# Two encoder layers in float32: when the heads' sums, the probabilities' parts, memory's sums and the weights' roundings are issued

## Chip, core and metric

The kernel runs on one core of a Trainium2 chip. The metric is the device time of one execution in microseconds; the median of several runs counts. The engines are TensorE (PE; its weight loads are PEld), VectorE (DVE), ScalarE (ACT), GpSimd (POOL) and SyncE (SP, which issues the DMAs here).

## What is computed

Two layers over 512 positions of 1024 values, and a final normalisation. Cut to what matters:

```python
for l in range(2):
    x = x + hybrid_mixer(rms_norm(x, norm_mix[l]), w_in[l], ...)      # 8 neighbourhood heads (8 x 16 window)
                                                                      # + 8 grouped-query heads, 2 key/value heads
    x = x + memory_cross_attention(rms_norm(x, norm_mem_q[l]), rms_norm(mem, norm_mem_kv[l]), ...)  # 4 heads, 256 tokens
    x = x + conv_ffn(rms_norm(x, norm_ffn[l]), ...)                   # SwiGLU, width-3 convolution, 2816 wide
return rms_norm(x, norm_final)

# the grouped-query heads: each query and key head is RMS-normalised, then rotated
g_q = apply_axial_rope(rms_norm(g_q, q_norm), cos, sin)
g_k = apply_axial_rope(rms_norm(g_k, k_norm), cos, sin)
```

## The kernel before

**Numbers in two parts.** All is float32. For a product each operand is split into a rounded high part and the low remainder, and three matmuls are made (`mm3`: high x high, high x low, low x high); attention probabilities and values use two parts stored side by side. A weight is loaded by SP into one of two `raw` tiles, rounded to `hi` by ACT (L265) and subtracted to `lo` by POOL, for a few by DVE (L266), in `emit_split`. `get_w` asks for the next weight and emits the splits of those up to two further on; `plan` fixes the order of weights. A PSUM result is split in `split_psum`: ACT rounds (L473), DVE subtracts (L474).

**Order.** TensorE's and SP's instructions keep the order in which they are written. Those of ACT, DVE and POOL are ordered by a planner that takes, among the steps it thinks ready, the one written first; `behind(n)` gives a step a place n instructions later (or earlier, when n is negative). `W_BEHIND` is 45 for most roundings of weights.

**Attention as a weave.** `weave` runs steps of the units (scores, normalise, transpose, values) with delays between them, and at each `None` a `Filler` runs pieces of other TensorE work, up to a quantum of nanoseconds (`NA_FILL`, `GQA_FILL`): input projections, grouped-query projections, the output projection of the neighbourhood heads (`out_na`), the memory keys and values, and the first rows of the closing product (`close_rows`). A piece ends at a `yield`, and each piece ticks `late`, which calls functions put off by so many pieces. `Counted` adds up the nanoseconds of matmuls that quanta are measured by; a matmul counts at least 107.

**Rotated heads.** `gqa_project` makes a group's projection in two pieces of 12 matmuls of 512 columns. `gqa_rope` scales it (L843, L844 on DVE) and squares it (L845 on ACT). Then, put off: `swap` (four DMAs that exchange rows); one piece later `rotate` (column sums of the squares on TensorE, the matmuls on `pairs`; L858 on DVE; the power -1/2, L864, and its copy, L865, on POOL; the addition L866 on POOL); two pieces later `norm` (four matmuls on `ident` that turn the copy); one piece later `split` (L876). The groups are k, 0, 1, v, 2, 3, where v has no rotation.

**PSUM.** Eight banks: four `mm`, two `sc` (scores), two `tr` (transposes, sums and small products).

**Memory.** `mem_stat`, in layer 0 alone, loads the memory tokens, squares them on ACT (L541), sums the squares of eight chunks on DVE by two reductions (L542) and an addition (L543), sums over partitions on TensorE, takes the power, and spreads the result (`mem_rep`, L556). `MEM_STEPS` says at which steps of the second attention its pieces, and those of `memory_prepare`, come.

**Closing rows.** The last product before a normalisation ends row by row. `Norm.close` adds the residual (L429), copies the row (L430), makes the next product's operand, high part on ACT (L439) and low part on DVE (L441), and squares the row (L445 on ACT, then L453 and L456, additions on POOL or DVE). `fold` adds the two parts of a head pair's output and puts off its split (L492 on ACT, L493 on POOL).

## Time and profile before

| what | value |
|---|---|
| median of 3 runs | 1382.12 us (1381.91 to 1383.89) |
| profiled execution | 1382.43 us, of which the span is 1380.3 us |
| mean granted TensorE clock | 0.994 |
| busy: PE, DVE, ACT, POOL | 1352.6, 862.9, 673.4, 701.9 us |
| chain that ended last | 91% PE |

The span runs from the first to the last instruction of the program. A row of a timeline reads: start, duration, engine, line, operation, out<-in, size, count, and in brackets the idle time of the engine before it with what ended it. A row of the waits reads: who waited, for whom, microseconds in total, how often, the longest. "L474" is line 474 of the kernel before.

### The profile page before, as it was taken

Reading aid. Unit: us, or ns where it says so; the run is one execution under the profiler, and the core shown is the slowest. Engines: PE = TensorE matmul, PEld = TensorE weight load, DVE = VectorE, ACT = ScalarE, POOL = GpSimd, SP = SyncE. Lnnn points to the kernel's source line nnn. Section 1 sums busy time; section 2 is a strip of 40 time slices with the busy share of each in tenths; the row PEclk is TensorE's granted clock in tenths of the full one; section 3 lists DMA queues with packets and bytes.
Section 4 is the critical chain, followed back from the end, with each engine's and each line's share of the span. In section 5 each row is a group of like instructions: output and inputs, shape, how many; then the busy total and the mean of one; then the engine's idle time right before and its main releaser. Section 6 shows DMA issues by size and latency. Waiting matters only on the chain.

```text
span 1380.3 us, 19215 instructions
## 1 busy us (share of the span) xinstructions
PE 1352.6 (98%) x7072; PEld 1155.5 (84%) x7072; DVE 862.9 (63%) x1522; ACT 673.4 (49%) x1255; POOL 701.9 (51%) x521
## 2 busy tenths in 40 slices
PE   9999899999999999999999999999999999999997
PEld 7898689888888888888888978897888888888897
DVE  6666766564886188268546557745748833861874
ACT  6765577464543243233546646755644423432441
POOL 2457676626444443443635577756364444444441
PEclk9999999999999999999999999999999999999999
DMA  6653312222333333332455531223133333333331
GB/s 215 203 146 85 99 47 77 92 61 77 107 93 93 106 92 88 109 94 87 121 140 171 139 106 55 72 72 102 53 96 96 92 104 95 90 94 107 91 94 62
DMA packets 218205, 138.83 MB, mean 101 GB/s; under 512 B 6016, under 2 KB 211072, under 8 KB 218112
## 3 DMA queue, kind: packets, MB, share of 16 engines
q1 hardware_dynamic: 217968, 137.60, 34.2%
q8 instruction: 56, 0.92, 0.3%
q14 instruction: 37, 0.30, 0.1%
q10 hardware_dynamic: 144, 0.00, 0.0%
HBM read 125.00 MB, written 2.10 MB: 92 GB/s over the span
## 4 chain that ended last, share of the span: by engine, by line
PE 91%; DVE 3%; ACT 2%; DMA 2%; POOL 1%; issue 1%; SPq 0%; DVEq 0%; ACTq 0%; POOLq 0%
PE mm L77 82%; PE sc L77 5%; PE tr L64 3%; PE tr L77 1%; DMA raw<-in_w_in 1%; ACT hi L265 1%; POOL lo L266 1%; DMA raw<-in_w_mem_q 1%; DVE xg L474 0%; DVE s L901 0%; DVE t L456 0%; DVE mm L429 0%; DVE t L542 0%; SPq L64 0%; DVE xT L430 0%
## 5 line engine op out<-in xcount | busy, mean ns | idle before, releaser
L266 POOL TENSOR_TENSOR lo<-raw,hi 128x1024 fp32r<-128x1024 f32 (+2 forms) x268 | 499.0, 1874 | 516.0 <-ACT hi L265 513.6
L77 PE MATMUL mm<-xg,hi 128*128 128x512 f32 x1920 | 594.3, 391 | 0.0
L77 PEld LDWEIGHTS mm<-xg,hi 128*128 128x128 f32 x1920 | 356.8, 188 | 71.9 <-ACT t L845 0.2
L265 ACT CAST hi<-raw 128x512 fp32r<-128x512 f32 (+2 forms) x276 | 224.2, 836 | 369.4 <-PE mm L77 301.9
L77 PE MATMUL mm<-xg,lo 128*128 128x512 f32 x960 | 373.8, 389 | 0.0
L77 PE MATMUL mm<-r,hi 128*128 128x512 f32 (+1 forms) x1144 | 333.1, 375 | 3.0 <-DVE xg L441 2.6
L77 PEld LDWEIGHTS mm<-r,hi 128*128 128x128 f32 x1144 | 208.3, 190 | 42.1 <-DVE xg L441 4.3
L1207 DVE SCALAR_TENSOR_TENSOR t<-t,par,t 128x7 f32<-128x7 f32 (+1 forms) x352 | 201.9, 641 | 34.0 <-ACT t L1200 34.0
L77 PE MATMUL mm<-r,lo 128*128 128x512 f32 (+1 forms) x572 | 213.7, 374 | 0.0
L77 PEld LDWEIGHTS mm<-xg,lo 128*128 128x128 f32 x960 | 180.2, 188 | 38.0
L77 PEld LDWEIGHTS mm<-r,lo 128*128 128x128 f32 x572 | 108.3, 189 | 19.1
L1192 DVE TENSOR_TENSOR t<-mm,rep 128x512 f32<-128x512 f32 x88 | 60.1, 687 | 78.0 <-PE mm L77 62.4
L480 POOL TENSOR_SCALAR t<-t,s 128x512 f32<-128x512 f32 (+1 forms) x112 | 66.2, 607 | 81.1 <-DVE s L752 42.3
L1213 DVE TENSOR_TENSOR r<-t,r 128x512 fp32r<-128x512 f32 x44 | 90.1, 2047 | 7.3 <-ACT r L1212 4.1
L1209 ACT ACTIVATE t<-t 128x512 f32<-128x512 f32 x44 | 27.9, 633 | 134.4 <-DVE t L1207 134.4
L1236 DVE TENSOR_TENSOR xT<-xT,mm 128x512 f32<-128x512 f32 x32 | 21.9, 685 | 106.8 <-PE mm L77 106.8
L77 PE MATMUL sc<-r,r 128*128 128x256 f32 (+1 forms) x352 | 72.5, 338 | 1.6 <-ACT t L903 1.6
L1200 ACT ACTIVATE t<-t,par 128x512 f32<-128x512 f32 x88 | 66.9, 806 | 3.3 <-DVE t L1192 3.3
L64 PE MATMUL tr<-ident,t 128*128 128x128 f32 x456 | 61.9, 274 | 4.8 <-DVE xg L474 1.7
L64 PEld LDWEIGHTS tr<-ident,t 128*128 128x128 f32 x456 | 52.3, 140 | 13.3 <-issue 3.5
L77 PE MATMUL mm<-r,r 128*128 128x256 f32 (+1 forms) x428 | 61.8, 297 | 0.0
L77 PEld LDWEIGHTS mm<-r,r 128*128 128x128 f32 x428 | 56.1, 191 | 2.4
(150 smaller groups left out, 1571.5 us busy)
## 6 DMA issues: line engine op xcount, KB each, us to landing
raw<-in_w_up SPq DMA_DIRECT2D x88, 512.0 KB, 3.7
raw<-in_w_in SPq DMA_DIRECT2D x33, 512.0 KB, 4.4
raw<-in_w_down SPq DMA_DIRECT2D x32, 448.0 KB, 3.6
raw<-in_w_mem_kv SPq DMA_DIRECT2D x16, 512.0 KB, 3.8
raw<-in_w_down SPq DMA_DIRECT2D x16, 512.0 KB, 4.0
r<-in_bias SPq DMA_DIRECT2D x16, 384.0 KB, 5.5
r<-r SPq DMA_DIRECT2D x22, 256.0 KB, 5.1
raw<-in_w_out SPq DMA_DIRECT2D x8, 512.0 KB, 3.6
```

What stands on the lines that cost most here:

```text
L64: return lambda *a, **k: self.tc.keep_in_program_order(op(*a, **k))
L77: return self.tc.keep_in_program_order(self.engine.matmul(out, lhsT, rhs, **k))
L265: act.copy(hi[:, k], raw[:, k])
L266: (POOL if eng[0] == "P" else DVE).tensor_sub(lo[:, k], raw[:, k], f(hi)[:, k])
L480: eng.tensor_scalar(e, e, sums[:, col : col + 1], 1.0, op0=ALU.mult, op1=ALU.mult)
L1192: DVE.tensor_mul(u, us[side], ffn.rep)
L1200: ACT.activation(cc, u, AF.Identity, bias=par[:, l, CB + ch : CB + ch + 1], scale=w[1])
L1207: DVE.scalar_tensor_tensor(cc[:, dst], u[:, src], wi, cc[:, dst], op0=ALU.mult, op1=ALU.add)
L1209: ACT.activation(cs[0], cs[0], AF.Silu)
L1213: DVE.tensor_sub(acts[j][1], cs[0], f(acts[j][0]))
L1236: DVE.tensor_add(xT[m], xT[m], pm)
```

## The change

Six things are edited. The rotated heads' sums, L858, the power and its copy move from `rotate` to `swap`. `split_psum` of both attentions' probabilities gets a place 20 instructions earlier, the split in `fold` one 60 earlier, the copy to `mem_rep` one 30 earlier. Memory's squares and sums get a place 60 later, each reduction is cut into four of 64 columns, the two halves become two pieces, and layer 0 has its own `MEM_STEPS`, in which the load comes a step earlier. While rows close (and, at the start, after the last square), the rounding of the weights `memq`, `up` and `k` is issued on ACT only after the operand of the row closed last (after the last square); this is an order of issue on that engine, not a wait for a result.

```diff
@@ -49,7 +49,7 @@
 GQA_FILL = [2300] * 16 + [3000] * 4
 MEM_FILL = [1, 1, 2, 2, 1, 3, 1, 3, 1, 3, 1]
 N_ROWS = 3
-MEM_STEPS = [0, 0, 1, 0, 1, 1, 1, 1, 1, 1, 1] + [0] * 9
+MEM_STEPS = [[0, 1, 0, 1, 1, 1, 1, 1, 1, 1, 1] + [0] * 9, [0, 0, 1, 0, 1, 1, 1, 1, 1, 1, 1] + [0] * 9]
 W_BEHIND, N_RAW, N_W, AHEAD, AHEAD_HELD, N_WARM, N_LATE, N_FIRST = 45, 2, 4, 2, 5, 8, 4, 4
 
 
@@ -232,6 +232,8 @@
 
     plan, raws, ready = [], [], []
     done = [0]
+
+    closed = []
 
     def raw_tile():
         key, loads, nk, ncol, eng = plan[len(raws)]
@@ -262,7 +264,8 @@
         with behind(W_BEHIND if done[0] and key[0] not in ("up", "down") else 0):
             for i in range(cuts):
                 k = slice(nk * i // cuts, nk * (i + 1) // cuts)
-                act.copy(hi[:, k], raw[:, k])
+                with tc.issue_after(closed[-1]) if closed and key[0] in ("memq", "up", "k") else nullcontext():
+                    act.copy(hi[:, k], raw[:, k])
                 (POOL if eng[0] == "P" else DVE).tensor_sub(lo[:, k], raw[:, k], f(hi)[:, k])
         ready.append((hi, lo))
 
@@ -428,21 +431,23 @@
 
             DVE.tensor_add(pm, pm, xT[c])
             DVE.tensor_copy(xT[c], pm)
-            self.operand(c, src=pm)
+            closed.append(self.operand(c, src=pm).ins)
             self.square(c)
+            if c == KC - 1:
+                closed.clear()
 
         def operand(self, c, act=ACT, src=None, dve=DVE, hi_only=False, lo_only=False):
             src = xT[c] if src is None else src
             g = par[:, self.l, self.gcol + c : self.gcol + c + 1]
             hi, lo = self.ops[c]
-            if not lo_only:
-                act.activation(hi, src, AF.Copy, scale=g)
+            e = None if lo_only else act.activation(hi, src, AF.Copy, scale=g)
             if not hi_only:
                 dve.scalar_tensor_tensor(lo, src, g, f(hi), op0=ALU.mult, op1=ALU.subtract)
+            return e
 
         def square(self, c, act=ACT, eng=None):
             sq = tmp((self.n,))
-            act.activation(sq, xT[c][:, self.cols], AF.Square)
+            e = act.activation(sq, xT[c][:, self.cols], AF.Square)
             eng = eng or (POOL if self.gcol is not None and c < KC - 1 else DVE)
             if self.acc is None:
                 self.acc = sq
@@ -454,6 +459,7 @@
                 self.acc = acc
             else:
                 eng.tensor_add(self.acc, self.acc, sq)
+            return e
 
         def stat(self, factor=1.0):
             pv = ps_t()
@@ -489,8 +495,9 @@
             DVE.tensor_add(o32[r], po[0:64, j], th[r, j])
 
         def split():
-            ACT.copy(out[0][:, cs], o32)
-            POOL.tensor_sub(out[1][:, cs], o32, f(out[0][:, cs]))
+            with behind(-60):
+                ACT.copy(out[0][:, cs], o32)
+                POOL.tensor_sub(out[1][:, cs], o32, f(out[0][:, cs]))
             done()
 
         late(1, split)
@@ -538,10 +545,14 @@
         acc = tmp((2, MEMN))
         for i in range(2):
             sq = rtile((4, MEMN), F32)
-            ACT.activation(sq, raw[i], AF.Square)
-            DVE.tensor_reduce(acc[:, i], sq.rearrange("p k n -> p n k"), axis=AX.X, op=ALU.add)
-        DVE.tensor_add(acc[:, 0], acc[:, 0], acc[:, 1])
-        yield
+            with behind(60):
+                ACT.activation(sq, raw[i], AF.Square)
+                for j in range(4):
+                    c = slice(64 * j, 64 * j + 64)
+                    DVE.tensor_reduce(acc[:, i, c], sq[:, :, c].rearrange("p k n -> p n k"), axis=AX.X, op=ALU.add)
+                if i == 1:
+                    DVE.tensor_add(acc[:, 0], acc[:, 0], acc[:, 1])
+            yield
         pv = ps_t()
         for b in range(MB):
             PE.matmul(pv[:, b : b + 1], acc[:, 0, b * P : (b + 1) * P], ones, start=True, stop=True)
@@ -553,7 +564,8 @@
         for b in range(MB):
             PE.matmul(pr[:, b * P : (b + 1) * P], mem_rstd[:, b : b + 1].to_broadcast([P, P]), ident,
                       start=True, stop=True)
-        ACT.copy(mem_rep, pr[:, :MEMN])
+        with behind(-30):
+            ACT.copy(mem_rep, pr[:, :MEMN])
         yield from memory_prepare(0, raw)
 
 
@@ -584,7 +596,9 @@
         if n[2] == "1":
             raws[c] = None
     for c in range(KC):
-        nn.square(c, ACT_IN_ORDER, DVE)
+        squared = nn.square(c, ACT_IN_ORDER, DVE)
+
+    closed.append(squared.ins)
 
 
     for l in range(DEPTH):
@@ -615,6 +629,7 @@
                         PE.matmul(pms[u], w[u][1][:, k], xg[k][0], start=False, stop=False)
                     continue
                 gemm_T(pms[u], w[u], xg, range(k0, k1), 0, KC - 1)
+            closed.clear()
             load_bias(0)
             load_parameters()
             mix.stat()
@@ -767,7 +782,8 @@
                     for c in range(2):
                         PE.transpose(tr[:, (2 * i + c) * P : (2 * i + c + 1) * P], es[j][:, i, c * P : (c + 1) * P], ident)
                 pt = rtile((2, S))
-                split_psum(pt[:, 0, :], pt[:, 1, :], tr)
+                with behind(-20):
+                    split_psum(pt[:, 0, :], pt[:, 1, :], tr)
                 pts.append(pt)
             na[u] = pts
 
@@ -848,9 +864,6 @@
                 xr = tmp()
                 for i in range(4):
                     SP.dma_start(xr[32 * i : 32 * i + 32], xs[32 * (i ^ 1) : 32 * (i ^ 1) + 32])
-                late(1, lambda: rotate(xr))
-
-            def rotate(xr):
                 pv = ps_t()
                 for b in range(NB):
                     PE.matmul(pv[:, 2 * b : 2 * b + 2], sq[:, b * P : (b + 1) * P], pairs, start=True, stop=True)
@@ -863,6 +876,9 @@
                 with behind(-40):
                     POOL.tensor_tensor(r, v, mhalf[:, : 2 * NB], op=ALU.pow)
                     POOL.tensor_copy(rows.rearrange("p (b d) -> p b d", d=HD), r.unsqueeze(2).to_broadcast([P, 2 * NB, HD]))
+                late(1, lambda: rotate(xr, rows))
+
+            def rotate(xr, rows):
                 POOL.tensor_add(xr, cc, xr)
                 late(2, lambda: norm(xr, rows))
 
@@ -923,7 +939,8 @@
                 for k in range(NB):
                     PE.transpose(tr[:, k * P : (k + 1) * P], es[j][:, k * P : (k + 1) * P], ident)
                 hi, lo = (v[:, :, ib, :] for v in gpt[u // 2][j])
-                split_psum(hi, lo, tr.rearrange("p (k n) -> p k n", n=P))
+                with behind(-20):
+                    split_psum(hi, lo, tr.rearrange("p (k n) -> p k n", n=P))
 
         gpo, whole = {}, [False] * 4
 
@@ -1044,7 +1061,7 @@
         ms = Filler(PE, late, mem_stat() if l == 0 else memory_prepare(l))
 
         def gqa_quanta(s):
-            ms.step(MEM_STEPS[s])
+            ms.step(MEM_STEPS[l][s])
             return [GQA_FILL[s]]
 
         weave(4 * NB, [(2, gqa_transpose_p), (1, gqa_normalise), (0, gqa_scores), (3, lambda u: gqa_values(u, 0)),
```

More of the change, by code (lines that the diff above doesn't have):

```diff
@@ L1 @@
-from contextlib import ExitStack, contextmanager
+from contextlib import ExitStack, contextmanager, nullcontext
 import numpy as np
```

## The prediction

> **What bounds it now.** I read the page first, then the list of TensorE's waits, then stage windows and timelines around each wait.

> ```profile
> span 1380.3 us, 19215 instructions
> PE 1352.6 (98%) x7072; PEld 1155.5 (84%) x7072; DVE 862.9 (63%) x1522; ACT 673.4 (49%) x1255; POOL 701.9 (51%) x521
> ```

> TensorE (PE) is busy 98%; only its 27.7 us of idle, and the time it runs slowly, can be won. TensorE's rows of the list of waits say where the idle lies (us in total, times, longest):

> ```profile
> PE mm L77 <- POOL t L865: 5.2, 2, 2.7
> PE mm L77 <- DVE xg L441: 2.6, 4, 1.2
> ...
> PE tr L64 <- DVE xg L474: 1.7, 1, 1.7
> PE sc L77 <- ACT t L903: 1.6, 3, 0.9
> PE tr L77 <- DVE t L543: 1.3, 1, 1.3
> ...
> PE tr L64 <- DVE s L909: 0.9, 1, 0.9
> PE tr L64 <- ACT mem_rep L556: 0.8, 1, 0.8
> ```

> The largest is the heads' power (L865's copy), once a layer. TensorE's timeline of layer 1 (start, duration):

> ```profile
> 822.08 0.40 PE L77 MATMUL mm<-r,lo 128*128 128x512 f32 x1
> 825.13 2.07 PE L77 MATMUL mm<-ident,t 128*128 128x128 f32 x8 [2.65 <-POOL t L865]
> 827.00 1.71 PE L77 MATMUL tr<-pairs,t 128*128 128x2 f32 x8
> ```

> In layer 0 the same pairs of groups took 1.16 and 0.95 us. The windows say why (engine columns PE, PEld, DVE, ACT, POOL, then PEclk):

> ```profile
> 145.60:148.90 3.30, 3.30 (x9) 2.52 (x9) 1.49 (x3) 1.10 (x2) 3.30 (x3) 0.50 1.08 364
> 824.90:831.60 6.70, 6.47 (x23) 5.89 (x24) 3.18 (x6) 1.32 (x3) 5.37 (x8) 0.50 0.90 280
> 838.00:842.00 4.00, 2.33 (x15) 1.86 (x14) 3.43 (x7) 3.58 (x10) 3.93 (x5) 1.00 0.01 2
> 150.00:172.00 22.00, 19.84 (x104) 16.08 (x104) 18.30 (x28) 13.84 (x29) 12.78 (x18) 1.00 0.17 48
> ```

> After each power wait the granted clock is 0.50: 3.30 us in layer 0 and 6.47 us of work in layer 1 at half speed, a hidden 1.65 + 3.24 = 4.9 us that no wait shows. The third window, with a wait of 1.67 us, stays at 1.00. So these two waits cost 5.25 + 4.9 = 10.1 us.

> **The sums and the power a piece sooner (+7.2 us).** The column sums (`pairs`), `v`, the power and its copy of each rotated group go from `rotate` to `swap`, one filler piece earlier: 12 matmuls of 512 columns, 2.7 us. The power (1.65 us) and copy (0.61 us) of group 2 then fall into POOL's 2.93 us idle stretch before 138.69 (layer 0) and 3.08 us before 819.02 (layer 1); the 5.25 us of wait and the 4.9 us of half clock go. No instruction is added; the four row-swapping DMAs keep their place, and POOL's addition of the swapped rows loses its place ahead of the power, which only `split`, three pieces on, needs.

> What is late next: group 3. Its piece after the projection holds no projection work, so its sums now stand behind only eight value matmuls (layer 0) or four scores (layer 1), about 1.0 us, and read the squares of L845:

> ```profile
> 137.99 1.14 ACT L265 CAST hi<-raw 128x512 fp32r<-128x512 f32 x2 [3.32 <-PE mm L77]
> 139.78 0.60 ACT L845 ACTIVATE t<-mm 128x512 f32<-128x512 f32 x1 [0.65 <-issue]
> ```

> The projection ended at about 138.2, L843 and L844 on DVE follow, and L845 starts after L844 in all ten groups: the squares come 2.1 us after the projection. New wait: 2.1 - 1.0 = 1.15 us a layer, -2.3 us. Behind it on TensorE stands everything, first scores or the output projection.

> A second new wait: counting the sums (4 x 107 ns in `Counted`) one run earlier moves pieces, which I followed through the quanta by hand. Two sums of layer 0 (groups k and 0) come to stand right before a transposing step. The sums take one of the two `tr` tiles until L858 has read it, and L858 ended 1.2 to 1.8 us after the sums began in layer 0, while sums plus the first four transposes take 1.3 us: between 0 and 0.5 us each, I take 0.3, -0.6 us. The other shifts only exchange equal TensorE work between steps of the second attention; I take nothing, covered by the same matmuls. Sum: 10.15 - 2.3 - 0.6 = +7.2.

> [...]

> **Memory's sums in eight (+2.4).** Two reductions of 1.95 us each (L542, 165.00 to 168.89) hold DVE; behind them queue the scores' maximum (TensorE waits 0.94 for L903) and the total L543 (1.26). Eight pieces of 64 columns cost 3.9 us plus six more starts; the smallest DVE steps (L858, eight columns) take 0.16, so about 0.9 us more. They hold DVE some 0.6 us at a time, and are queued 60 places later. Best end: both waits go, +2.2; worst: all 4.8 us are left until TensorE asks for the total, and it waits 4.8 instead of 2.2, -2.6. The load moves a step up, its two DMAs past at most the two `mem_kv` loads issued at 141.57 and 142.20, whose weights are used only near 199. The last window decides: DVE is busy 18.30 of 22.00 us, 2.2 of which were waits, so it fits; I take +1.7. `mem_rep`'s copy, 30 places forward, no longer stands behind a rounding: 0.83, I take 0.7.

> **Probabilities' parts in front (+1.8).** At 838.42 transposes wait 1.67 us for a `tr` tile because L685 (1.39 us) went before L474 on DVE; at 894.38, 0.90 us because L901, L1008 did. Twenty places reach past those. I take 2.2 of 2.57. L901 and so L903 come later by up to 0.7 us, where L903 already holds scores (0.34 and 0.33): -0.4, ends 0 and -1.0. The 0.57 us at 812 waits for the value heads' `turn`, whose split is not moved, and stays.

> **Outputs' splits in front (+0.3).** They take 0.34 us of wait away (L493, at 249.2); what they pass on ACT and POOL waits at most 0.41 and 0.74 us.

> **Roundings behind closing rows (+2.0).**

> ```profile
> 252.62 1.05 ACT L265 CAST hi<-raw 128x1024 fp32r<-128x1024 f32 x1 [4.07 <-DMA raw<-in_w_mem_q]
> 253.57 0.68 ACT L439 ACTIVATE xg<-mm,par 128x512 fp32r<-128x512 f32 x1
> ```

> ACT sits idle 4 us waiting for weights that nobody wants yet, while L439's input (L429) was there at 251.0. TensorE then waits for the row's PSUM: 0.69 + 0.35 in layer 0, 1.21 + 0.35 in layer 1, 2.60 in all. Behind rows 3 and 5 the roundings are later; the second memory query weight then has its rounding at 263 to 264, its low part (2.4 us on POOL) at 266.4, or up to 269 behind two square additions (1.3 each), and is wanted at 269.5. So +2.6 at best, -1.5 at worst; I take 2.0. Feed-forward weights have some 4 us of slack, the next layer's key weight 3, counted the same way.

> **The start (+1.2).** The rounding of the fourth weight (L265, 1.14 us at 16.39) goes behind six squares. The sum of squares ends sooner (wait on L456, 0.74), and the power L404, now behind two low parts on POOL, should come first, since those weights load later (0.66). Ends +1.4 and, if they stay in front, -1.5.

> **Sum.** 7.2 + 2.4 + 1.8 + 0.3 + 2.0 + 1.2 = 14.9 us. Some is given back, because the same DVE and POOL work must fit into less time: in 150 to 172 DVE would be 92% busy (18.3 of 19.8), and POOL has 3.1 us idle between 819 and 840 plus the 2.3 moved away for 6.2 us of shortening. Nearest rows are the 0.3 to 0.9 us waits that stay on L903 and L480; I take 3 us, ends 0 and 6. Net 11.9 us from the profiled 1382.43 (1380.3 span, 2.1 around it), which is 0.3 above the median of 1382.12: 1370.2, say 1370.

> **Rivals.** *The half clock stays.* The new 1.15 us wait is followed by sums that stream almost nothing (0.85 us), 2.0 us together: between the 1.67 that kept the clock and the 2.60 that lost it. Then 4.9 us are not won: 1375. For it: the sums did not lift the clock at 827. Against: it is nearer to 1.67. 0.18.

> *The places do nothing.* `behind` is a preference among ready steps, not an order; where a step wasn't ready in the planner's view, nothing moves. Parts, splits and `mem_rep` stay (2.8 us): 1373. 0.08.

> *Given back entirely*: DVE's latency sets the steps and the waits come back as L901 and L903. 92% busy speaks for it, the 5.4 us of idle DVE between 144 and 153 against: 1381. 0.06.

> *Slower: the roundings starve.* POOL is busy 9.79 of 10 us in 255 to 265. If the delayed low parts fall behind all six square additions (7.8 us), the second memory query weight is ready near 274 and TensorE waits 4.7 us plus up to 3.3 us of half clock, in both layers: 16 us lost, 10 won elsewhere: 1388. It decides above 5 us a closing; needed is an order that puts additions of rows not yet closed first, hence 0.06.

> **Numbers.** The forecast, 1370, has 0.62. Every term at its best end (7.8 + 3.0 + 2.6 + 0.3 + 2.6 + 1.4 = 17.7) and nothing given back reach 1364; the half clock together with memory's sums at their worst reaches 1379. About 0.2%, 2.8 us, is what runs of this kernel can tell from nothing (they spread over 2.0). Faster 0.62 + 0.18 + 0.08 = 0.88; same 0.06; slower 0.06.

> **What would show it.** Right: no TensorE wait on L865 and PEclk 1.00 around both places; a new wait of about 1.2 us on L845 at each; L542 rows of some 0.6 us, no wait on L543 above 0.5; L439 ahead of L265 at the closings. Wrong: PEclk 0.50 there still; TensorE waiting for POOL's low parts after a closing; longer waits on L903.

## The result: 2.5 us faster, a fifth of the forecast

The median of the changed kernel is 1381.03 us (20 runs, 1377.48 to 1383.63) against 1383.57 us of the kernel before in the same comparison (20 runs, 1381.46 to 1385.95): ratio 0.9985, 95% interval 0.9978 to 0.9992. The forecast was 1370.0, with a range from 1364 to 1379; it started from the 1382.12 of three runs, 1.45 under the 20 runs here. The profiled execution took 1380.32 us, of which the span is 1378.4. Lines of the changed kernel are shifted: L845 became L861, L865 L878, L474 L480, L480 L486, L441 L445, L903 L919, L265 L268, L414 L417, L542 L552, L671 L686.

The head of the page and TensorE's rows of the list of waits, after:

```profile
span 1378.4 us, 19211 instructions
PE 1352.8 (98%) x7072; PEld 1156.2 (84%) x7072; DVE 865.2 (63%) x1528; ACT 674.2 (49%) x1255; POOL 701.7 (51%) x521
...
PE tr L64 <- DVE xg L480: 2.7, 1, 2.7
PE tr L77 <- ACT t L861: 2.4, 2, 1.2
PE mm L77 <- DVE xg L445: 1.6, 4, 0.4
...
PE sc L77 <- ACT t L919: 1.3, 2, 1.0
...
PE sc L77 <- DVE r L686: 1.1, 1, 1.1
...
PE tr L64 <- DVE s L925: 0.9, 1, 0.9
```

The 5.2 us on the power's copy are gone, and the two new waits on the squares are there with the forecast 1.2 us each. What was not forecast is the top row: 2.7 us on a low part of the second attention's probabilities. The windows, columns as before, add the other surprise: TensorE still runs at half clock in three places.

```profile
143.10:146.50 3.40, 3.40 (x14) 3.02 (x13) 2.48 (x6) 0.62 (x1) 2.95 (x3) 0.50 0.74 211
163.60:167.00 3.40, 3.40 (x10) 2.62 (x9) 2.90 (x6) 1.32 (x4) 1.53 (x2) 0.50 0.01 2
825.80:829.20 3.40, 3.40 (x13) 3.04 (x12) 0.81 (x2) 0.17 (x1) 3.40 (x5) 0.50 0.82 258
150.00:172.00 22.00, 18.39 (x88) 14.73 (x87) 17.54 (x34) 14.20 (x31) 15.71 (x22) 0.92 0.13 36
```

That is 3 x 3.41 = 10.2 us at 0.50, as much as before (3.41 + 6.83). Two of the three stand behind the new 1.2 us waits, the third behind the 2.7 us wait.

The memory stretch explains that wait. DVE's timeline of the changed kernel (start, duration, then in brackets the idle time before):

```profile
157.62 0.61 DVE L552 TENSOR_REDUCE t<-r 128x64 f32<-128x256 f32 x1
158.15 0.68 DVE L480 TENSOR_TENSOR xg<-tr,xg 128x512 fp32r<-128x512 f32 x1
158.74 3.11 DVE L552 TENSOR_REDUCE t<-r 128x64 f32<-128x256 f32 x6
161.78 0.67 DVE L480 TENSOR_TENSOR xg<-tr,xg 128x512 fp32r<-128x512 f32 x1
```

and TensorE's in the same stretch:

```profile
157.95 0.39 PE L77 MATMUL mm<-r,lo 128*128 128x512 f32 x1
159.23 0.66 PE L64 MATMUL tr<-ident,t 128*128 128x128 f32 x4 [0.89 <-POOL t L486]
162.60 0.63 PE L64 MATMUL tr<-ident,t 128*128 128x128 f32 x4 [2.72 <-DVE xg L480]
```

Six of the eight pieces stand in one row of 3.1 us between the two low parts (L480) of one unit. The next transposes need the `tr` tile that the second low part frees, and wait until it ends. Here the small pieces let nothing in between: the second low part is queued behind all six, and starts at 161.78, when their row (158.74 and 3.11 us) is at its end.

### The profile page after: what moved, and what is told of

It is laid out like the page before. It is cut to its first block, busy times and chain, and to the rows that moved or that the text cites. A ratio compares the mean times of both kernels' runs of the same rounds, so it can differ in the third digit from the quotient of the medians.

```text
span 1378.4 us, 19211 instructions
## 1 busy us (share of the span) xinstructions
PE 1352.8 (98%) x7072; PEld 1156.2 (84%) x7072; DVE 865.2 (63%) x1528; ACT 674.2 (49%) x1255; POOL 701.7 (51%) x521
## 4 chain that ended last, share of the span: by engine, by line
PE 88%; DVE 4%; ACT 3%; DMA 2%; POOL 1%; issue 1%; SPq 0%; DVEq 0%; ACTq 0%; POOLq 0%
PE mm L77 79%; PE sc L77 5%; PE tr L64 3%; PE tr L77 1%; POOL lo L269 1%; DMA raw<-in_w_in 1%; DVE mm L432 1%; ACT hi L268 1%; DVE xT L433 1%; DMA raw<-in_w_mem_q 1%; DMA raw<-in_w_mem_o 0%; DVE s L917 0%; DMA r<-in_w_in 0%; ACT t L1104 0%; ACT t L919 0%
## 5 line engine op out<-in xcount | busy, mean ns | idle before, releaser
L77 PE MATMUL mm<-xg,hi 128*128 128x512 f32 x1920 | 594.4, 391 | 0.4 <-ACT t L861 0.4
L77 PEld LDWEIGHTS mm<-xg,hi 128*128 128x128 f32 x1920 | 356.7, 188 | 72.0 <-ACT t L861 0.6
L268 ACT CAST hi<-raw 128x512 fp32r<-128x512 f32 (+2 forms) x276 | 224.1, 836 | 350.5 <-PE mm L77 277.7
L77 PE MATMUL mm<-xg,lo 128*128 128x512 f32 x960 | 373.7, 389 | 0.0
L77 PE MATMUL mm<-r,hi 128*128 128x512 f32 (+1 forms) x1144 | 333.1, 375 | 1.9 <-DVE xg L445 1.6
L77 PEld LDWEIGHTS mm<-r,hi 128*128 128x128 f32 x1144 | 208.1, 189 | 40.7 <-DVE xg L445 3.2
L77 PE MATMUL mm<-r,lo 128*128 128x512 f32 (+1 forms) x572 | 213.7, 374 | 0.0
L77 PEld LDWEIGHTS mm<-xg,lo 128*128 128x128 f32 x960 | 180.2, 188 | 38.1
L77 PEld LDWEIGHTS mm<-r,lo 128*128 128x128 f32 x572 | 108.2, 189 | 19.1
L486 POOL TENSOR_SCALAR t<-t,s 128x512 f32<-128x512 f32 (+1 forms) x112 | 66.3, 609 | 84.0 <-DVE s L925 44.2
L77 PE MATMUL sc<-r,r 128*128 128x256 f32 (+1 forms) x352 | 73.0, 340 | 2.4 <-ACT t L919 1.3
L64 PE MATMUL tr<-ident,t 128*128 128x128 f32 x456 | 62.7, 274 | 7.5 <-DVE xg L480 2.7
L64 PEld LDWEIGHTS tr<-ident,t 128*128 128x128 f32 x456 | 52.1, 141 | 16.8 <-issue 3.9
L77 PE MATMUL mm<-r,r 128*128 128x256 f32 (+1 forms) x428 | 62.0, 297 | 0.0
L77 PEld LDWEIGHTS sc<-r,r 128*128 128x128 f32 x352 | 52.0, 192 | 7.6 <-ACT t L919 2.5
```

Source lines behind the costliest of these rows:

```text
L64: return lambda *a, **k: self.tc.keep_in_program_order(op(*a, **k))
L77: return self.tc.keep_in_program_order(self.engine.matmul(out, lhsT, rhs, **k))
L268: act.copy(hi[:, k], raw[:, k])
L486: eng.tensor_scalar(e, e, sums[:, col : col + 1], 1.0, op0=ALU.mult, op1=ALU.mult)
```

## Experiments

All were timed in five rounds beside the kernel before, whose median was 1383.56, 1383.39 and 1383.51 us in the three comparisons. The second comparison ran on another chip, so kernels of different comparisons are set against each other by their ratios. Each kernel numbers its lines anew.

**The change without memory's sums in eight** (the two reductions and `MEM_STEPS` as before):

```diff
-            with behind(60):
-                ACT.activation(sq, raw[i], AF.Square)
-                for j in range(4):
...
+            ACT.activation(sq, raw[i], AF.Square)
+            DVE.tensor_reduce(acc[:, i], sq.rearrange("p k n -> p n k"), axis=AX.X, op=ALU.add)
```

> The changed kernel with memory's sums alone put back (two reductions, the load a step later); all else of the change stays. Theory 'pieces in a row': six of the eight pieces run one after the other on DVE ahead of the low part of a transposed probability, and TensorE's 2.72 us and 0.89 us waits near 160 and the half clock from 163.6 come from that; they go, the two waits of before (0.94 and 1.26) come back, and the time is 2 to 3 us under the changed kernel, about 4.5 us under the kernel before (ratio 0.9967). Rival 'DVE is full there whatever the pieces': the waits near 160 stay in another form, and the time is that of the changed kernel (0.9985).

1377.54 us, ratio 0.9955 (0.9942 to 0.9967). The wait of 2.72 us and the half-clock window at 163.6 are gone; one window of 3.41 us is left, at 143.74. Against the expectation, the two waits of before (0.94 and 1.26) did not come back: 0.39 and 0.44 stand there. So the sums in eight, forecast to gain 1.7 (2.4 with `mem_rep`'s copy, which stays in this kernel), cost 3.5 us inside the change (1381.03 - 1377.54). DVE's timeline has the two whole reductions behind both low parts of a unit:

```profile
160.71 0.69 DVE L480 TENSOR_TENSOR xg<-tr,xg 128x512 fp32r<-128x512 f32 x1 [0.31 <-ACT xg L479]
...
161.91 0.68 DVE L480 TENSOR_TENSOR xg<-tr,xg 128x512 fp32r<-128x512 f32 x1
...
163.11 3.97 DVE L549 TENSOR_REDUCE t<-r 128x256 f32<-128x1024 f32 x2
```

Memory's edit holds several things: the cut, a place 60 later, two pieces for one, and a load one step earlier. Which of them brought the reductions ahead of a low part was not tried apart.

**The last group's sums left a piece later** (groups k, 0, 1 and 2 moved, group 3 not):

```diff
+                if g != 3:
+                    power(rows)
...
             def rotate(xr, rows):
+                if g == 3:
+                    power(rows)
                 POOL.tensor_add(xr, cc, xr)
```

> The changed kernel in which the last group of heads (group 3) alone keeps its column sums and power one piece later, as before; the other four groups stay a piece sooner. Theory 'the squares come too late for group 3': the two waits on the squares (1.18 and 1.24 us) go and the clock stays full around both places: 2.4 + 3.4 us less, minus up to 1 us a layer if group 3's power is then late for its own spread; 3.5 to 5.5 us under the changed kernel (ratio to before 0.995 to 0.996). Rival 'the power again': TensorE waits 2 us or more on group 3's power, the clock halves there, and nothing is won (0.9985).

1383.45 us, ratio 1.0004 (0.9995 to 1.0013): where 3.5 to 5.5 us were expected, the change's whole gain is lost. TensorE's waits:

```profile
PE tr L64 <- DVE xg L480: 5.2, 4, 2.1
PE mm L77 <- POOL r L508: 4.5, 1, 4.5
...
PE mm L77 <- POOL t L883: 1.3, 1, 1.3
```

The waits on the squares are gone, as expected, but POOL does group 3's power, two rows of probabilities and the addition of the swapped rows (147.33 to 151.49) ahead of the low part L508 of the neighbourhood heads' last output, and the output projection waits 4.54 us for it. The waits on the low parts L480 grow as well, from 2.7 to 5.2 us. Group 3 belongs in the change.

**The heads' sums and power alone**, on the kernel before:

```diff
-                late(1, lambda: rotate(xr))
-
-            def rotate(xr):
                 pv = ps_t()
...
+                late(1, lambda: rotate(xr, rows))
+
+            def rotate(xr, rows):
                 POOL.tensor_add(xr, cc, xr)
```

> The kernel before with the heads' sums and power a piece sooner and nothing else. If the prediction's term holds with its two new waits and the half clock staying for one window of 3.4 us a layer: 5.25 - 2.4 - 0.6 of waits and 4.9 - 3.4 of clock, 3.7 us under before (ratio 0.9973). If the whole gain of the change came from elsewhere: no difference. If the earlier sums disturb the transposes of layer 0 by more than thought: 1 to 2 us (0.9990).

1377.84 us, ratio 0.9959 (0.9947 to 0.9972): 5.7 us where 3.7 were expected, more than twice the whole change. Both power waits are replaced by the same two on the squares (1.18 and 1.24), and half clock falls from 10.2 to 6.8 us. The waits of the memory stretch change as well, without any edit there: 0.94 on L903, 1.26 on L543 and 0.83 on `mem_rep` have become 0.86, 0.41, 0.44 and 0.28; that the sooner heads shift the steps around it is the likely reason, not a shown one. In the two profiles that is 5.2 - 2.4 = 2.8 us of waits, 1.7 of half clock and 1.0 in the memory stretch, 5.5 in all; and the 1.0 was booked in the prediction under memory's sums. The spans of these two profiles differ by 4.1 only: the waits on L441 grew from 2.6 to 3.2, and at the start the clock rose at 6.48 us instead of 5.63. The 5.7 rest on the medians.

**The closings alone**, on the kernel before:

> The kernel before with the roundings of weights queued behind the closing rows, without the one at the start, and nothing else. Prediction's term: TensorE's four waits on L441 (0.69, 0.35, 1.21, 0.35) nearly vanish, 2 us (ratio 0.9986). Rival 'DVE is the next in the chain': the row's operand on ACT then waits for DVE's copy of the row, the four waits end at 0.43, 0.35, 0.43, 0.35, and 1 us is won (0.9993).

1383.52 us, ratio 1.0 (0.9991 to 1.0009). The edit does what it says, as ACT's timeline shows:

```profile
253.07 0.69 ACT L443 ACTIVATE xg<-mm,par 128x512 fp32r<-128x512 f32 x1 [3.81 <-DVE xT L433]
253.66 0.62 ACT L450 ACTIVATE t<-xT 128x512 f32<-128x512 f32 x1
```

ACT has no rounding ahead of the operand any more, and still idles 3.81 us, now for DVE, which does two additions (251.06) and a copy (252.36 to 253.04) first. The operand reads the sum, not the copy, and yet starts only when the copy of the same row has ended. Counted from the first addition, because the two profiles are 0.7 us apart here, it starts after 2.0 us instead of 3.2 (250.33 to 253.57 before). The waits on its low part (L445) fall from 2.60 to 1.56 us, as the rival had it, and a new one of 1.15 us stands at 285.3, in front of the memory attention's transposes, so that nothing is won.

**Memory's sums in eight alone**, on the kernel before:

> The kernel before with one edit alone: memory's sums in eight pieces and its steps (load in step 1, sums in steps 3 and 4); everything else as before. Theory (the pieces stand in a row on DVE ahead of a low part that TensorE waits for, whatever the rest of the change does): about 3 us slower than before, 1386 to 1387, because taking the same edit out of the whole change gave 3.5 us (1381.0 to 1377.5); in the trace one TensorE wait of over 2 us on xg of L474 with at least five L539-L542 pieces of 0.57 us back to back ahead of it, between 155 and 170 us. Rival (the loss came only from where the sooner heads put this stretch): within 1 us of before, 1383 to 1384.5, with no wait of over 1.5 us there that before lacks.

1385.36 us, ratio 1.0020 (1.0010 to 1.0029): slower by itself, by 2.0 us where 3 were expected. DVE's timeline, and then TensorE's:

```profile
159.38 3.15 DVE L545 TENSOR_REDUCE t<-r 128x64 f32<-128x256 f32 x6
162.45 0.68 DVE L474 TENSOR_TENSOR xg<-tr,xg 128x512 fp32r<-128x512 f32 x1
```
```profile
163.27 0.63 PE L64 MATMUL tr<-ident,t 128*128 128x128 f32 x4 [2.46 <-DVE xg L474]
```

The same six in a row and a wait of 2.46 us behind them, without the heads' edit. The rival, that the sooner heads had put the stretch there, falls.

**The eight pieces emitted in four steps**, on the whole change:

```diff
+            for j in range(4):
+                c = slice(64 * j, 64 * j + 64)
+                with behind(60):
+                    DVE.tensor_reduce(acc[:, i, c], ...)
...
+                if j % 2:
+                    yield
```

> The whole change, with the eight pieces of memory's sums spread over four steps, two in each (steps 2 to 5; the load in step 0, the power in step 6, the row factors in step 7). Theory (the loss is the six pieces in a row, 3.5 us of DVE ahead of the low part): the TensorE wait of 2.72 us on xg of L480 near 163 us falls under 1 us, and 2 to 3 us come back, 1378 to 1379. Rival (DVE's added work as such, 8 x 0.57 = 4.6 us against 3.9, and the squares before them): nothing comes back, 1380.5 to 1382, with waits of the same sum in other places between 150 and 175 us.

1381.74 us, ratio 0.9989 (0.9980 to 0.9998): nothing came back, and by the expectation's words that spoke for the rival. DVE's timeline shows that the edit did not do what it was made for:

```profile
157.56 4.24 DVE L553 TENSOR_REDUCE t<-r 128x64 f32<-128x256 f32 x8
```

The planner put all eight in one row ahead of both low parts of the unit, and TensorE waits 2.28 us at 163.2. Steps written apart aren't steps queued apart. So this run could not tell the two theories apart; the next one could.

**The pieces queued behind the low part**, on the whole change, same pieces, same steps:

```diff
+                    with tc.issue_after(lows[-1]):
                         DVE.tensor_reduce(acc[:, i, c], sq[:, :, c].rearrange("p k n -> p n k"), axis=AX.X, op=ALU.add)
```

(`lows` holds the low parts, L474 of before, in the order in which they are written.)

> The whole change, with the same eight pieces in the same two steps, but each queued on DVE behind the last low part of the probabilities (L480) that was issued before it. Theory (the loss is the place of the pieces, six in a row of 3.1 us ahead of the second low part): the TensorE wait of 2.72 us on xg of L480 at 162.6 us falls to 0.7 us or less, the half-clock window at 163.6 us goes, and about 3 us come back, 1377.5 to 1378.5 (the changed kernel: 1381.0; without the sums in eight: 1377.5). Rival (the pieces' DVE time, or the squares ahead of them on ACT, is the loss wherever they stand): 1380.5 to 1382, with TensorE waits that sum to the same between 155 and 175 us.

1377.23 us, ratio 0.9954 (0.9942 to 0.9967): 3.8 us came back where about 3 were expected. DVE's timeline:

```profile
158.69 0.68 DVE L481 TENSOR_TENSOR xg<-tr,xg 128x512 fp32r<-128x512 f32 x1
159.28 2.18 DVE L554 TENSOR_REDUCE t<-r 128x64 f32<-128x256 f32 x4
...
161.46 0.67 DVE L481 TENSOR_TENSOR xg<-tr,xg 128x512 fp32r<-128x512 f32 x1
```

The second low part ends at 159.4 instead of 162.4; the wait on it and the half clock at 163.6 are gone, and what is left is 1.20 us on the exponentials at 166.4. The place of the pieces was the loss, not their work. Against the two whole reductions (1377.54) the well-placed pieces bring nothing that can be measured.

**The probabilities' parts alone**, on the kernel before:

> The kernel before with the probabilities' parts in front alone (both calls of split_psum, 20 places). Theory (a wait on a part turns into a wait on the exponentials behind it): 1383 to 1384, within 0.1% of before; the wait on L474 of 1.67 us in layer 1 becomes one of about 1 us on the exponentials (L903), the one of 0.90 us on the reciprocal (L909) stays. Rival (the prediction's term): 1.8 us less, 1381.7.

1383.43 us, ratio 1.0 (0.9991 to 1.0009). The total was as the theory said, but not for its reason, as two of TensorE's rows of the list of waits show:

```profile
PE tr L64 <- DVE xg L474: 1.7, 1, 1.7
...
PE tr L64 <- DVE s L910: 0.9, 1, 0.9
```

Neither wait turned into another; both stayed. The 20 places changed the order on ACT and DVE near 70 us and near 896 us alone; at 838 us, where L685 goes ahead of L474, it is that of before. That the planner had L685 ready first is the likely reason, not a shown one. In the changed kernel, with all the other edits, the 1.67 us did become 0.97 on the exponentials, which stand behind a weight's rounding on ACT (837.32 to 838.45); with the heads alone the 1.67 us stays.

**The last group's squares first**, on the change without the sums in eight, with the rounding of the last `outn` weight queued behind them:

```diff
+                if g == 3:
+                    sqs.append(ACT.activation(sq, pm, AF.Square).ins)
                 DVE.scalar_tensor_tensor(xs, pm, gain, gtab[0][:, 1], op0=ALU.mult, op1=ALU.mult)
```

> The changed kernel without the sums in eight (1377.5 on this chip's last comparison), and the squares of the last group of heads (L861 of after) put ahead of its two products on DVE, with the rounding of the last outn weight queued behind them. Theory (the waits of 1.18 and 1.24 us on these squares are what is left of the heads' cost, and the half-clock window of 3.41 us at 143.7 us follows them): both waits under 0.3 us, no half-clock window between 140 and 150 us, 1377.5 - 1.2 - 1.2 - 1.7 = 1373.4. Rival 1 (the clock halves all the same): the waits go and the window stays, 1375.1. Rival 2 (DVE's products, now 0.65 us later, are next): new waits of about 1 us on the products' rows (L882, L892), 1377 or more.

1376.91 us, ratio 0.9958 (0.9946 to 0.9969), against 0.9955 of the same kernel without this edit: no difference that the runs can tell, where 4 us were expected. Both waits on the squares are gone, but a half-clock window stands at 147.79. TensorE's timeline, and then POOL's, say what is next:

```profile
147.96 0.79 PE L77 MATMUL mm<-r,hi 128*128 128x512 f32 x1 [1.71 <-POOL r L510]
```
```profile
143.52 1.65 POOL L878 TENSOR_TENSOR s<-s,mhalf 128x8 f32<-128x8 f32 x1
145.41 1.27 POOL L883 TENSOR_TENSOR t<-t,t 128x512 f32<-128x512 f32 x1 [0.24 <-DMA t<-t]
146.64 1.27 POOL L510 TENSOR_TENSOR r<-t,r 128x512 fp32r<-128x512 f32 x1
```

The new wait is one of POOL's order. The addition L883 now stands ahead of the low part L510; without this edit that low part (L508 there) went first, at 145.30, and the addition followed. ACT's high part of the same output also comes later, at 145.07 instead of 144.10. The rows' DMAs, which wait for DVE's product, cost POOL 0.24 us. So the total is near what the second rival (the later products are next) said, but the row is another one, and only a small part of its wait is the products'. DVE did not read the projection while ACT squared it: it idled until the square ended (L859 starts at 140.57, the square L858 at 139.87 and takes 0.60). In the changed kernel it was the other way round: the square L861 starts at 141.06, when the second product L860 (140.29 and 0.74 us) has ended. In each of the two kernels the one that went second began when the other had ended; why is not shown.

**The start's rounding behind the row factors' copy**, on the change without the sums in eight:

```diff
-        ACT.copy(rep, pr[:, : n * P])
+        reps.append(ACT.copy(rep, pr[:, : n * P]).ins)
...
+                first = reps if n == 6 else closed if key[0] in ("memq", "up", "k") else []
+                with tc.issue_after(first[-1]) if first else nullcontext():
```

> The changed kernel without the sums in eight (1377.5), and the rounding of the third query weight in layer 0, which waits for its DMA until 29.4 us, queued behind the copy of the row factors (L417). Theory (the start's gain is given back because that copy stands behind the rounding): the copy runs at 28.3 to 28.6 us instead of 30.5, the DVE chain starts 1.9 us sooner, and the TensorE wait at 38 to 39.8 us (1.14 and 0.39 in the changed kernel) goes: about 1 us less, 1376.5. Rival (the loads' landing sets this stretch whatever is ahead of it): the copy is sooner and TensorE waits for a weight instead, 1377.5.

1376.32 us, ratio 0.9948 (0.9936 to 0.9960), 1.2 us under the 1377.54 without the repair. The two intervals overlap; but the three kernels with this repair (the two below as well) have ratios of 0.9948, 0.9946 and 0.9942, those without it and without the row of pieces 0.9955, 0.9958 and 0.9954. ACT's timeline, first of the changed kernel, then of this one:

```profile
29.42 1.14 ACT L268 CAST hi<-raw 128x512 fp32r<-128x512 f32 x2 [1.96 <-DMA raw<-in_w_in]
30.47 0.58 ACT L417 COPY rep<-tr 128x512 f32<-128x512 f32 x1
```
```profile
28.11 0.59 ACT L418 COPY rep<-tr 128x512 f32<-128x512 f32 x1 [0.73 <-PE tr L77]
29.58 1.15 ACT L269 CAST hi<-raw 128x512 fp32r<-128x512 f32 x2 [0.88 <-DMA raw<-in_w_in]
```

In the change, the start's two waits (0.74 and 0.66) did go, and TensorE was 1.07 us ahead at 27.4. But the copy that feeds DVE's chain stood behind a rounding that waits for its weight until 29.4 us in both kernels, and TensorE gave the lead back at 38.4 in one wait of 1.14 us on L686. With the repair that wait is 0.36 us. How much the repair brings hangs on when TensorE gets there: in the profile of the kernel without the sums in eight the 1.14 us are missing too; there the clock rose at 10.62 us instead of 6.57, and TensorE was 1.2 us later at 25 us.

**Two combinations.** The start's repair with the squares first:

> The changed kernel without the sums in eight, with the repaired start and the last group's squares ahead of its products. Theory: the squares' 0.6 us (1377.5 to 1376.9) and the start's 1.2 us (to 1376.3) add up, 1375.7, and a half-clock window stays near 146 us behind a new TensorE wait of 1.7 us on the low part of the window attention's last output (L502 or L510). Rival (the squares' gain is within what the runs scatter): 1376.3 to 1377.

1376.19 us, ratio 0.9946 (0.9933 to 0.9958): nothing over the start's repair alone. The granted clock stayed full from 4.6 us to 1366 us; the expected window near 146 us was not there, though the wait of 1.72 us on L510 was.

The whole change with the pieces behind the low parts and the start's repair:

> The whole change with the pieces queued behind the low parts and the start's rounding queued behind the row factors' copy. Theory: the two repairs add up, 3 us for the pieces and 1.2 us for the start: 1376 to 1377, 0.5% under before, the same as the changed kernel without the sums in eight and with the repaired start (1376.3); so the eight pieces bring nothing of their own. Rival (once out of the way, the pieces bring the 1.7 us that the prediction gave them): 1374.5.

1375.20 us, ratio 0.9942 (0.9930 to 0.9955): the fastest here, 8.3 us under before and 5.8 under the change. Together the two repairs bring 5.8 us where 3.8 and 1.2 were seen singly; the runs do not tell this from a plain sum. The 1.1 us that it is under the start's repair alone are no proof that the pieces pay, for its profile had no half-clock window beside the heads, with the same waits there.

## Why the prediction was wrong, point by point

**The heads (+7.2 forecast, 5.7 measured, interval 3.9 to 7.3).** Right in mechanism and in the rows that came next. The term that failed inside it is the 4.9 us of half clock: the rival "the half clock stays" described it, and had 0.18. The prediction reasoned from the length of a wait (1.67 kept the clock, 2.60 lost it); by the traces the length alone did not decide: 1.18 us were followed by 0.50 in the change (at 143.10) and by 1.00 in the fastest kernel, below. Of the 4.9 us, 1.7 were won in the profile of the heads alone and none in that of the change. The 0.6 us set aside for two `tr` tiles did not show: with the heads alone TensorE has no wait near the sums of k and 0 (99.01 and 108.18). In part the lost half clock was made up for by the 1.0 us that left the memory stretch with the heads.

**Memory's sums (+1.7 forecast, +2.4 with `mem_rep`; 2.0 lost alone, 3.5 lost in the change).** This is the step that failed, the largest miss of a single term and the one that turned a gain into a loss. It weighed the cost as DVE time against DVE's idle in a window of 22 us and took the pieces as singles ("some 0.6 us at a time"). It never asked which instruction stands next behind them in DVE's queue. 3.1 us in a row ahead of one low part cost 2.72 us of wait, and 1.7 us of half clock behind it. Inside the change the loss, by the medians, was beyond its worst end, -2.6. That end was thought of as a wait for the total, not for a low part.

**Parts (+1.8 forecast, 0 measured alone).** The rival "the places do nothing" held for this term.

**Closings (+2.0 forecast, 0 measured alone).** Mis-sized: the waits fell by 1.0, and a wait of 1.15 us in the memory attention took that back. The step took the row's sum, there at 251.0, for all that the operand needs; with the closings alone the operand started 0.03 us after DVE's copy of that row (253.07 against 253.04). That copy ended at 252.31 in the kernel before, 1.3 us ahead of ACT's rounding (253.67).

**Start (+1.2 forecast, none left at 39.7 us in the change).** The waits went as reasoned, and the gain was given back at the next obstacle in ACT's order, the rounding at 29.42, worth about 1 us when removed. The term also hung on one profile: the wait of 0.74 us on L456 is in none of the four other kernels that keep the start of before (heads, closings, parts and sums alone), and that of 0.66 us on L404 is 0.67, 0.62, 1.04 and absent in them.

**Outputs' splits (+0.3).** The wait stayed (0.35 at 250.3); not tried alone.

**Sum.** Heads 5.7; all else but the sums 0.3 (1377.84 to 1377.54); the sums -3.5: 2.5 us, the measured gain. It comes out by construction, since each term is the step from one median to the next, and 0.3 is within what the runs scatter. Against the forecast of 14.9 the heads are 1.5 short, the sums 5.2, and all the small terms together 5.7: parts, splits, `mem_rep`, closings and start were forecast at 6.0. The 3 us that the prediction held back as "given back" cover about half of the small terms and nothing of the loss.

## What to carry to other kernels

Cutting a long step into pieces did not help here while the pieces stood in a row: six of them, 3.11 us, cost a wait of 2.72 us. Read in the timeline which instruction comes next behind the row of pieces, and tie them to it if it matters (3.8 us came back here). A step that was moved ahead in one engine's order gained no more here than the distance to the next obstacle, on this engine or on its partner: the closings' operand came 1.2 us sooner (2.0 us behind the row's first addition instead of 3.2), up to the end of DVE's copy. Price an edit by the second-latest input, not by the wait that it removes. Where one edit carries the gain and others are added to it, time the one alone: here it was more than twice as good as the whole.

## What the hardware showed

```profile
141.40 1.05 PE L77 MATMUL tr<-pairs,t 128*128 128x2 f32 x8 [1.18 <-ACT t L864]
```
```profile
142.30:146.00 3.70, 3.70 (x22) 3.21 (x22) 3.23 (x7) 0.93 (x2) 2.78 (x3) 1.00 0.67 183
```

In the change the wait and the sums stood in one such stretch, from 139.69 to 143.10, with 4.5 matmuls' worth of columns, and the clock was 0.50 from 143.10. That the stretches fell otherwise around the sums of the fastest kernel, so that none was as poor, is the author's estimate from these counts; it is not shown.

**The pieces cost little.** Eight reductions of 64 columns took 4.24 us in a row (four steps, at 157.56), where the two whole ones took 3.89 (kernel before, 165.00 to 168.89). In the changed kernel each took 0.57 to 0.61 us, and in the row of six each starts 0.07 to 0.08 us before the one ahead of it has ended.
